# Taking the first four column tiles of a decoder layer K-tile by K-tile, and summing the squares of x on ScalarE

## The chip, the cores and the metric

The kernel runs on one core of one Trainium2 chip. The core has five engines, each with its own instruction stream in a fixed order: PE (TensorE, the matrix unit; PEld is its weight load), DVE (VectorE), ACT (ScalarE), POOL (GpSimd) and SP (SyncE, which here only issues loads). An instruction starts when those ahead of it on its engine have started and the semaphores that it waits for have come. The metric is the device time of one execution in microseconds (us). Profile rows name an instruction by its line in the kernel and by the names of the tiles that it writes and reads.

## The reference, cut to what matters

One layer of a hybrid decoder on x of 256 tokens by 2048 features, all float32:

```python
h = rms_norm(x, ln_mix_pre)
q, k, v, z, xbc, dt_raw = jnp.split(h @ w_in, splits, axis=-1)
attn = moba_attention(q, k, v, rel_bias)
ssm = mamba2_mixer(z, xbc, dt_raw, ...)          # conv of xbc, softplus of dt, chunked state space
x = x + rms_norm(concatenate([attn, ssm]) @ w_out, ln_mix_post)
h = rms_norm(x, ln_ffn_pre)
gate, up = jnp.split(causal_depthwise_conv(h @ w_ffn_up, ...), [FFN_HIDDEN], axis=-1)
x = x + rms_norm((gelu(gate) * up) @ w_ffn_down, ln_ffn_post)
```

`rms_norm` divides each token by the root of the mean of its squares over the 2048 features, plus 1e-6. What matters here is the start: `h @ w_in` for the last 512 columns of xbc (B and C of the state space) and for the 16 columns of dt.

## The kernel before

**Precision.** Each float32 operand of a large product is split into a rounded part (hi, made on ACT) and the exact rest (lo, made on DVE); a product is hi\*hi + lo\*hi + hi\*lo. The weights come in *units* of 128 x 1024 values (512 KB). `Weights.split` loads a unit into `raw` on SP's queue (L64), casts it to `whi` on ACT (L65) and subtracts on DVE for `wlo` (L66). There are four buffers of each; PE must be done with a unit before the cast of the fourth unit after it. `take` hands out the next unit, `fetch` splits one more, and `tick`, once after each unit that PE uses, calls `fetch` and then whatever was put off by `defer(n, ...)` until n more units.

**Activations.** x arrives transposed (`xT`, features on the partitions) in 16 K-tiles of 128 features by 256 tokens (128 KB each), into `xr`. `load_x` splits each, times the norm's weight, into `hT` (ACT L180, DVE L181). The root mean square itself is applied to the products later, so it isn't needed at the start.

**Column tiles.** A column tile is 128 columns of w_in for all 256 tokens in one PSUM bank: for each K-tile a *pair* of matmuls, `whi` against hi and lo together (L186, 512 columns) and `wlo` against hi (L187, 256). The first four tiles (`pab`: two from one PSUM pool, two from the other) are B and C. A unit holds eight K-tiles of one tile. `cols_group` takes the four first units side by side: K-tiles 0 to 3 of each of the four tiles, then 4 to 7 of each. The four units with K-tiles 8 to 15 come after, one tile at a time. Behind the group stand the 32 small matmuls `pd` for dt (L385, L386) on `wd`, the split weights of the 16 time-step columns. The order of instructions on each engine is settled when the program is built, by a scheduler that moves independent work; on PE it has put pd ahead of the second half of the four tiles.

**First loads.** The table `START` sets their order on SP's queue: single K-tiles of x, then pairs, between quarters and halves of the first four units, then `wdr` (time-step weights) and the last K-tiles; small tables (`hv`, `mch`, `cst`, `rb`, `oh`) follow. At the very start PE runs 22 matmuls on zeros (L323, `WARM`).

**Sums of squares.** GpSimd squares `xr` in four groups of four K-tiles into `sq` and adds them up (L372 to L377, nine instructions). When the first unit of v has been used, `token_rms` sums over the partitions with two small matmuls (`pms`, L399), and DVE and GpSimd make 1/sqrt of it (`rsa`, `rsy`, `rsq`, `rr`; `mean_rsqrt`, `rsqrt`).

**After it** come v (`rows_chunk`, matmuls of L266 to L268), eight column tiles of x of the state space, z, attention, the output projection and the feed-forward part; their code is the same in both kernels.

Of the kernel before, what the change touches and what calls it, by code (L numbers as in the profile page):

```python
# [19 lines left out]
P = 128  # L20
# [17 lines left out]
WARM = 22  # L38

# order of the first loads: (x, K-tile, count), (unit, from column block, to column block), time steps  # L40
START = [("x", 0, 1), (0, 0, 2), ("x", 1, 1), (0, 2, 4), ("x", 2, 2), (1, 0, 4), (2, 0, 4), ("x", 4, 2),
         (3, 0, 4), ("x", 6, 2), (0, 4, 8), (1, 4, 8), ("x", 8, 2), (2, 4, 8), (3, 4, 8), ("x", 10, 2),
         ("d",), ("x", 12, 4)]
# [3 lines left out]
# layout of the flat vector of row parameters  # L47
# [7 lines left out]
class Weights:  # L55
    """The weight units in the order of their use, fetched and split ahead of it."""
# [21 lines left out]
    def begin(self, n):  # L78
        """The first n units, for fetching piece by piece."""
        self.fetched = n  # L80
        return [self.tiles(i) for i in range(n)]

    def fetch(self):
        """One more unit into the pool, and those before it that have a place of their own."""
        while self.fetched < len(self.units):
            i = self.fetched
            self.fetched += 1
            self.split(*self.tiles(i), slice(0, UE))
            if i not in self.place:
                return  # L90
# [8 lines left out]
def decoder_layer(ctx, tc, x, xT, win, wdt, wout, wup, wdown, relb, vec, cols, mconv, fconv,  # L99
# [23 lines left out]
    def rsqrt(a, meanwhile=None):  # L123
        """1 / sqrt, element by element of a few columns."""
# [14 lines left out]
    def mean_rsqrt(src, inv):  # L139
        """rsqrt(src * inv + EPS)"""  # L140
# [5 lines left out]
    def early_sum(parts):  # L146
        """The mean square's share of the first three chunks, and EPS."""
# [5 lines left out]
    def late_rsqrt(part, early, meanwhile):  # L153
        """With the share of the last chunk."""
# [4 lines left out]
    def along_tokens(dst, rs):  # L159
        """Columns of one value per token -> dst[every partition, 256 tokens]."""  # L160
# [10 lines left out]
    def split_evac(dst, k, ts, ps):  # L171
        """PSUM -> rounded part and the exact rest, for K-tiles k and token columns ts."""
# [4 lines left out]
    def split_scaled(dst, k, ts, src, w):  # L177
        """The same with a factor per feature."""
# [4 lines left out]
    def cols_part(ps, w, aT, k, j):  # L183
        """K-tile k, the j-th of the unit: ps[128 columns of W, 256 tokens] in two summands."""
# [5 lines left out]
    def cols_tok(ps, w, aT, k, j, t):  # L190
        """The same for one token tile; the last matmul for both, once the bank is begun."""
# [8 lines left out]
    def cols_sum(dst, ps):  # L200
        """Both summands of a tile, and the root mean square of the tokens."""
# [26 lines left out]
    def cols_group(pss, aT):  # L228
        """Tiles side by side, where the activations still come in."""
        w = [ws.take() for _ in pss]  # L230
        for js in (range(4), range(4, 8)):
            for i, ps in enumerate(pss):
                for j in js:
                    cols_part(ps, w[i], aT, j, j)
                if js[-1] == 7:
                    tick()
        for ps in pss:
            w = ws.take()
            for j in range(8):
                cols_part(ps, w, aT, 8 + j, j)  # L240
            tick()

    def cols_pair(pss, aT):
        """Two tiles together, the first token tile ahead of the second, which still comes in."""
# [16 lines left out]
    def rows_part(ps, w, aT, k0, t, first, last):  # L261
        """ps[128 tokens of t, 512 columns] += two K-tiles from k0 on."""
# [8 lines left out]
    def rows_chunk(pss, aT, kts, first=True, last=True, done=None):  # L271
        """The units of the K-tile pairs kts, for both token tiles."""
# [10 lines left out]
    def rows_staggered(pss, aT, kts, done, late, first=True):  # L283
        """The last chunk: eight units token tile by token tile, four of them with their own place."""
# [41 lines left out]
    with ExitStack() as mctx:  # L326
# [3 lines left out]
        with ExitStack() as actx:  # L330
# [3 lines left out]
            # x^T * ln, split; the root mean square is applied to the products  # L334
# [9 lines left out]
            wd = ax.tile([P, KT, 2 * SH], F32R, name="wd")  # L344

            def load_wd():
                nc.sync.dma_start(out=wdr, in_=wdt)
                nc.scalar.copy(wd[:, :, :SH], wdr)
                nc.vector.tensor_tensor(wd[:, :, SH:], wdr, f32(wd[:, :, :SH]), op=ALU.subtract)

            starts = ws.begin(4)
            for kind, *what in START:
                if kind == "d":
                    load_wd()
                elif kind == "x":
                    load_x(*what)
                else:
                    ws.split(*starts[kind], slice(what[0] * P, what[1] * P))
            hv = ax.tile([P, 3, SH], F32, name="hv")
            nc.sync.dma_start(out=hv, in_=row_bcast(V_HEADS, 48))  # L360
            mch = ax.tile([P, 12, 5], F32, name="mch")
            nc.sync.dma_start(out=mch, in_=mconv)
            nc.sync.dma_start(out=cstt, in_=consts)
            rb = ax.tile([33, H], F32, name="rb")
            nc.sync.dma_start(out=rb, in_=relb)
            oh = ax.tile([33, RELW], F32, name="oh", tag="rel", bufs=1)
            nc.sync.dma_start(out=oh, in_=onehot)

            sq = pers.tile([P, 4, 4, S], F32, name="sq", tag="xt", bufs=1)
            for g in range(4):  # L370
                xg = xr[:, g * 4:g * 4 + 4, :]
                nc.gpsimd.tensor_tensor(sq[:, g], xg, xg, op=ALU.mult)  # L372
                if g > 0:
# [597 lines left out]
```

## Time and profile before

| what | value |
|---|---|
| time, median of 3 runs | 1156.71 us (1155.48 to 1157.04) |
| span of the profiled execution | 1153.8 us |
| instructions | 15725 |
| mean granted clock of PE | 0.989 |
| loaded from HBM | 212.39 MB |

The page gives no device time for the profiled execution beside its span; the three timed runs are 1.7 to 3.2 us longer than that span. Of the span's 40 equal slices the first is the one in which PE is least busy apart from the last, and both its clock and the loads are below those of the rest:

```profile
PE   6998999999999899999999999999999999999996
...
POOL 6015122000001500000000000000000000000001
PEclk8999999999999999999999999999999999999999
```

Each digit is the busy share of a slice of 28.8 us in tenths (PEclk: the granted clock in tenths).

### The profile page before, as it was taken

The page shows a single profiled execution, that of the slowest core. Times are in us where ns is not written, and L with a number is a line of the kernel's source. Part 1 is how long each engine was busy: PE and PEld are TensorE (multiplying, and loading weights), DVE is VectorE, ACT ScalarE, POOL GpSimd, SP SyncE. Part 2 cuts the span into 40 slices and gives each one's busy share as a digit, 9 for nine tenths or more (in the row PEclk, how much of TensorE's full clock was granted, in tenths as well). Part 3 has the DMA queues.
Part 4 walks back from the last instruction along what each step waited for, and adds up shares of the span by engine and source line. Part 5 has one row for each costly group of instructions (what it writes and reads, how often), then busy time and mean ns, then how long its engine had stood idle before and what let it go on. Part 6 is the DMA issues. An engine that isn't in the chain of part 4 may idle for free.

```text
span 1153.8 us, 15725 instructions
## 1 busy us (share of the span) xinstructions
PE 1127.2 (98%) x5878; PEld 959.5 (83%) x5878; DVE 806.7 (70%) x1226; ACT 584.0 (51%) x901; POOL 84.9 (7%) x66
## 2 busy tenths in 40 slices
PE   6998999999999899999999999999999999999996
PEld 4877888888888798888888888888888888888885
DVE  8678876766646788778777744447787787775563
ACT  5455544545445466555555544335555555554450
POOL 6015122000001500000000000000000000000001
PEclk8999999999999999999999999999999999999999
DMA  5657644555477455555555555555555555555562
GB/s 196 204 178 243 194 149 147 177 170 165 164 310 237 144 176 198 183 189 192 185 185 189 191 183 190 193 183 187 193 186 184 192 190 183 188 190 188 185 217 73
DMA packets 61189, 215.55 MB, mean 187 GB/s; under 512 B 7247, under 2 KB 8840, under 8 KB 60472
## 3 DMA queue, kind: packets, MB, share of 16 engines
q1 hardware_dynamic: 58408, 204.74, 53.0%
q0 software_dynamic: 1696, 8.60, 2.1%
q10 hardware_dynamic: 1008, 1.20, 0.3%
q8 instruction: 46, 0.75, 0.3%
q14 instruction: 31, 0.25, 0.1%
HBM read 212.39 MB, written 2.13 MB: 186 GB/s over the span
## 4 chain that ended last, share of the span: by engine, by line
PE 93%; DVE 3%; DMA 2%; issue 1%; SPq 0%; POOL 0%; ACT 0%; DVEq 0%; POOLq 0%; ACTq 0%
PE pa L186 36%; PE pa L187 19%; PE pa L266 8%; PE pa L268 8%; PE pa L267 8%; PE ph L267 4%; PE ph L266 4%; PE ph L268 4%; DVE wlo L66 2%; DMA raw<-in_win_dram 1%; PE pa L194 1%; DMA rows<-acd 1%; PE py L557 1%; DVE rows L533 1%; DMA acd<-acr 0%
## 5 line engine op out<-in xcount | busy, mean ns | idle before, releaser
L66 DVE TENSOR_TENSOR wlo<-raw,whi 128x1024 fp32r<-128x1024 f32 (+2 forms) x381 | 472.8, 1243 | 269.1 <-ACT whi L65 268.5
L65 ACT CAST whi<-raw 128x1024 fp32r<-128x1024 f32 (+2 forms) x381 | 395.0, 1038 | 459.4 <-PE pa L186 171.4
L186 PE MATMUL pa<-h,whi 128*128 128x512 f32 x1376 | 483.3, 394 | 0.0
L187 PE MATMUL pa<-h,wlo 128*128 128x256 f32 x1376 | 389.2, 283 | 0.0
L186 PEld LDWEIGHTS pa<-h,whi 128*128 128x128 f32 x1376 | 258.4, 188 | 59.6
L187 PEld LDWEIGHTS pa<-h,wlo 128*128 128x128 f32 x1376 | 258.7, 188 | 0.0
L186 PE MATMUL pa<-hT,whi 128*128 128x512 f32 x416 | 152.0, 404 | 0.0
L187 PE MATMUL pa<-hT,wlo 128*128 128x256 f32 x416 | 119.5, 287 | 7.4 <-DVE wlo L66 7.3
L186 PEld LDWEIGHTS pa<-hT,whi 128*128 128x128 f32 x416 | 79.9, 192 | 17.7
L798 DVE SCALAR_TENSOR_TENSOR cfc<-cfu,fcv,cfc 128x255 f32<-128x255 f32 (+1 forms) x176 | 84.6, 481 | 4.5 <-ACT cfc L796 1.5
L187 PEld LDWEIGHTS pa<-hT,wlo 128*128 128x128 f32 x416 | 80.1, 193 | 8.5 <-DVE wlo L66 8.5
L266 PE MATMUL pa<-whi,gT 128*128 128x512 f32 x176 | 69.4, 395 | 0.0
L268 PE MATMUL pa<-whi,gT 128*128 128x512 f32 x176 | 69.4, 395 | 0.0
L267 PE MATMUL pa<-wlo,gT 128*128 128x512 f32 x176 | 69.4, 394 | 0.0
L127 POOL TENSOR_TENSOR rsy<-rsa,mhalf 128x1 f32<-128x1 f32 (+1 forms) x10 | 7.8, 780 | 788.7 <-DVE rsa L156 732.1
L268 PE MATMUL ph<-whi,gT 128*128 128x512 f32 x160 | 63.1, 395 | 0.0
L267 PE MATMUL ph<-wlo,gT 128*128 128x512 f32 x160 | 63.1, 395 | 0.0
L266 PE MATMUL ph<-whi,gT 128*128 128x512 f32 x160 | 63.1, 395 | 0.0
L796 ACT ACTIVATE cfc<-cfu,fcv 128x256 f32<-128x256 f32 x88 | 52.5, 597 | 1.4 <-DVE cfu L795 1.4
L266 PE MATMUL pa<-whi,hT 128*128 128x512 f32 x128 | 52.4, 410 | 0.0
L267 PE MATMUL pa<-wlo,hT 128*128 128x512 f32 x128 | 50.5, 395 | 0.0
L268 PE MATMUL pa<-whi,hT 128*128 128x512 f32 x128 | 50.5, 395 | 0.0
(237 smaller groups left out, 1234.9 us busy)
## 6 DMA issues: line engine op xcount, KB each, us to landing
raw<-in_wup_dram SPq DMA_DIRECT2D x176, 512.0 KB, 3.5
raw<-in_wdown_dram SPq DMA_DIRECT2D x88, 512.0 KB, 3.5
raw<-in_win_dram SPq DMA_DIRECT2D x84, 512.0 KB, 3.5
raw<-in_wout_dram SPq DMA_DIRECT2D x32, 512.0 KB, 4.3
rows<-acd POOLq DMA_DIRECT2D x4, 512.0 KB, 7.7
xt<-in_x_dram POOLq DMA_DIRECT2D x2, 1024.0 KB, 7.6
raw<-in_win_dram SPq DMA_DIRECT2D x7, 256.0 KB, 6.4
xr<-in_xT_dram SPq DMA_DIRECT2D x5, 256.0 KB, 5.8
```

The source lines that it names most:

```text
L65: nc.scalar.copy(hi[:, s], raw[:, s])
L66: nc.vector.tensor_tensor(lo[:, s], raw[:, s], f32(hi[:, s]), op=ALU.subtract)
L186: nc.tensor.matmul(ps, w[0][:, s], aT[:, k, :, :], start=(k == 0), stop=False)
L187: end[0] = nc.tensor.matmul(ps[:, :S], w[1][:, s], aT[:, k, 0, :], start=False, stop=(k == KT - 1)).ins
L194: nc.tensor.matmul(both, w[0][:, s], aT[:, k, :, tok(t)], start=(t == 0 and k == 0), stop=False)
L266: nc.tensor.matmul(ps, a, w[0][:, s], start=(first and j == 0), stop=False)
L267: nc.tensor.matmul(ps, a, w[1][:, s], start=False, stop=False)
L268: end[0] = nc.tensor.matmul(ps, b, w[0][:, s], start=False, stop=(last and j == 1)).ins
L533: nc.vector.tensor_scalar(seg[:, i, :], seg[:, i, :], nacs[:, t, h:h + 1], 0.0, op0=ALU.add, op1=ALU.min)
L557: nc.tensor.matmul(py[:, i * 64:(i + 1) * 64], rows[:, t, g, i, :], xcs[t, g][:, i * 64:(i + 1) * 64], start=True, stop=True)
L796: nc.scalar.activation(c, u, AF.Identity, scale=wv[:, 2:3], bias=wv[:, 3:4])
L798: nc.vector.scalar_tensor_tensor(c[:, sh:], u[:, :S - sh], wv[:, 2 - sh:3 - sh], c[:, sh:], op0=ALU.mult, op1=ALU.add)
```

## The change

Comments and docstrings are dropped, and line numbers shift by up to eleven. Besides that:

- `cols_first` takes the place of `cols_group`. The first eight units are laid out anew on the host: each holds two K-tiles for all four tiles. PE goes through the units in turn, and in each through K-tile 2u for tiles 0 to 3, then K-tile 2u + 1.
- The first loads follow that order. K-tiles 0 and 1 of x come singly, each ahead of its half of unit 0; units 1 to 3 come whole, each behind its two K-tiles of x. K-tiles 8 and 9 follow; the last six come two at a time behind the fetches of units 4 to 6.
- `load_rest`, after unit 7 is fetched: x again, row by row (tokens on the partitions, two loads of 1 MB), squared in place on ACT with the sum over the features as a second output (`ssx`); then the time-step weights and the small tables.
- GpSimd's nine instructions and the two matmuls of `pms` go; `token_rms` reads `ssx`.
- The warm-up has 16 matmuls in place of 22.

```diff
-WARM = 22
-START = [("x", 0, 1), (0, 0, 2), ("x", 1, 1), (0, 2, 4), ("x", 2, 2), (1, 0, 4), (2, 0, 4), ("x", 4, 2),
...
+WARM = 16
...
-    def cols_group(pss, aT):
-        w = [ws.take() for _ in pss]
-        for js in (range(4), range(4, 8)):
-            for i, ps in enumerate(pss):
-                for j in js:
-                    cols_part(ps, w[i], aT, j, j)
-                if js[-1] == 7:
-                    tick()
-        for ps in pss:
+    def cols_first(pss, aT, after):
+        for u in range(KT // 2):
             w = ws.take()
-            for j in range(8):
-                cols_part(ps, w, aT, 8 + j, j)
+            for j in range(2):
+                for i, ps in enumerate(pss):
+                    cols_part(ps, w, aT, u * 2 + j, j * 4 + i)
             tick()
+            after(u)
...
+            xsq = pers.tile([P, NT, D], F32, name="xsq", tag="xt", bufs=1)
+            ssx = ax.tile([P, NT], F32, name="ssx")
+            def load_rest():
+                for t in range(NT):
+                    nc.sync.dma_start(out=xsq[:, t, :], in_=x[0, tok(t), :])
+                    nc.scalar.activation(xsq[:, t, :], xsq[:, t, :], AF.Square,
+                                         accum_out=ssx[:, t:t + 1])
                 nc.sync.dma_start(out=wdr, in_=wdt)
                 nc.scalar.copy(wd[:, :, :SH], wdr)
                 nc.vector.tensor_tensor(wd[:, :, SH:], wdr, f32(wd[:, :, :SH]), op=ALU.subtract)
+                for dst, src in ((hv, row_bcast(V_HEADS, 48)), (mch, mconv), (cstt, consts),
+                                 (rb, relb), (oh, onehot)):
+                    nc.sync.dma_start(out=dst, in_=src)
...
+            for k in range(2):
+                load_x(k, 1)
+                ws.split(*starts[0], slice(k * 512, k * 512 + 512))
+            for u in range(1, 4):
+                load_x(2 * u, 2)
+                ws.split(*starts[u], slice(0, UE))
+            load_x(8, 2)
+            def after(u):
+                if u < 3:
+                    load_x(10 + 2 * u, 2)
+                elif u == 3:
+                    load_rest()
...
-            for g in range(4):
-                xg = xr[:, g * 4:g * 4 + 4, :]
-                nc.gpsimd.tensor_tensor(sq[:, g], xg, xg, op=ALU.mult)
-                if g > 0:
-                    nc.gpsimd.tensor_tensor(sq[:, 0], sq[:, 0], sq[:, g], op=ALU.add)
...
-                pms = psum("pms")
-                for t in range(NT):
-                    nc.tensor.matmul(pms[:, t:t + 1], s0[:, 0, tok(t)], ones, start=True,
-                                     stop=True)
-                nc.vector.tensor_copy(rr, mean_rsqrt(pms[:, :NT], 1.0 / D))
+                nc.vector.tensor_copy(rr, mean_rsqrt(ssx, 1.0 / D))
...
-    win = np.concatenate([xbc[16:24:2], xbc[17:24:2], rows(w_in[:, 2048:3072]), xbc[:16],
+    win = np.concatenate([rows(w_in[:, 5120:5632]), rows(w_in[:, 2048:3072]), xbc[:16],
```

Where the instructions stand now is shown at three places. The first is PE, right behind the warm-up, before the change (the numbers are those of buffers: 215 to 218 are the banks of the four tiles):

```order
L186 MATMUL pab_215<-hT_100,whi_115 128x512
L187 MATMUL pab_215<-hT_100,wlo_116 128x256
...
L186 MATMUL pab_216<-hT_100,whi_118 128x512
L187 MATMUL pab_216<-hT_100,wlo_119 128x256
...
L186 MATMUL pa_217<-hT_100,whi_121 128x512
L187 MATMUL pa_217<-hT_100,wlo_122 128x256
```

and in the changed kernel (167 to 170 are the banks of the four tiles):

```order
L181 MATMUL pab_167<-hT_94,whi_115 128x512
L181 MATMUL pab_168<-hT_94,whi_115 128x512
L181 MATMUL pa_169<-hT_94,whi_115 128x512
L182 MATMUL pab_167<-hT_94,wlo_116 128x256
L182 MATMUL pab_168<-hT_94,wlo_116 128x256
L182 MATMUL pa_169<-hT_94,wlo_116 128x256
L181 MATMUL pa_170<-hT_94,whi_115 128x512
L182 MATMUL pa_170<-hT_94,wlo_116 128x256
```

Before, four pairs of one tile use one unit, and the next tile needs another; now the first half of one unit serves all four tiles. The pairs of a tile's later K-tiles are left out ahead.

The second place is ACT from the last feature splits on, before the change (`wd` are the time-step weights, `dsb` the copy of pd, `bc` the copies of the finished tiles):

```order
L180 ACTIVATE hT<-xr,cw 128x256 x2
L348 CAST wd<-wdr 128x16x16
L180 ACTIVATE hT<-xr,cw 128x256 x4
L405 ACTIVATE aneg<-hv 128x16
L65 CAST whi<-raw 128x1024
L389 COPY dsb<-pd 32x256
L65 CAST whi<-raw 128x1024 x3
L202 COPY bc<-pab 128x256
L65 CAST whi<-raw 128x1024
L202 COPY bc<-pab 128x256
```

and in the changed kernel, from the last feature split on:

```order
L175 ACTIVATE hT<-xr,cw 128x256 x2
L60 CAST whi<-raw 128x1024
L348 ACTIVATE xsq,ssx<-xsq 128x2048
L197 COPY bc<-pab 128x256 x2
L197 COPY bc<-pa 128x256
L348 ACTIVATE xsq,ssx<-xsq 128x2048
L351 CAST wd<-wdr 128x16x16
L197 COPY bc<-pa 128x256
L394 ACTIVATE aneg<-hv 128x16
L60 CAST whi<-raw 128x1024 x2
L382 COPY dsb<-pd 32x256
```

The cast of the time-step weights has moved from among the feature splits to behind the copies of three finished tiles and the second Square. The third place is DVE at the same point, before the change:

```order
L181 SCALAR_TENSOR_TENSOR hT<-xr,cw,hT 128x256 x2
L349 TENSOR_TENSOR wd<-wdr,wd 128x16x16
L181 SCALAR_TENSOR_TENSOR hT<-xr,cw,hT 128x256 x2
L404 TENSOR_SCALAR mch<-mch 128x60
L181 SCALAR_TENSOR_TENSOR hT<-xr,cw,hT 128x256 x2
L406 TENSOR_SCALAR aneg<-aneg 128x16
L66 TENSOR_TENSOR wlo<-raw,whi 128x1024 x4
L203 TENSOR_TENSOR bc<-pab,bc 128x256
```

and in the changed kernel, from the rest of unit 7 on:

```order
L61 TENSOR_TENSOR wlo<-raw,whi 128x1024
L198 TENSOR_TENSOR bc<-pab,bc 128x256 x2
L198 TENSOR_TENSOR bc<-pa,bc 128x256
L393 TENSOR_SCALAR mch<-mch 128x60
L138 TENSOR_SCALAR rsa<-ssx 128x2
L128 TENSOR_TENSOR rsq<-rsy 128x2
L352 TENSOR_TENSOR wd<-wdr,wd 128x16x16
L198 TENSOR_TENSOR bc<-pa,bc 128x256
L129 TENSOR_TENSOR rsq<-rsq,rsa 128x2
L395 TENSOR_SCALAR aneg<-aneg 128x16
```

The rest of wd now follows the sums of three tiles and the first two steps of the mean's root, of which `rsq` reads what GpSimd has made of `rsa`. On PE pd stands right behind the four tiles, and the first unit of v behind pd. From the third unit of v on the order on every engine is as before.

More of the change, by code (lines that the diff above doesn't have):

```diff
@@ L37 @@
 SPLB = 4
-WARM = 22
-START = [("x", 0, 1), (0, 0, 2), ("x", 1, 1), (0, 2, 4), ("x", 2, 2), (1, 0, 4), (2, 0, 4), ("x", 4, 2),
-         (3, 0, 4), ("x", 6, 2), (0, 4, 8), (1, 4, 8), ("x", 8, 2), (2, 4, 8), (3, 4, 8), ("x", 10, 2),
-         ("d",), ("x", 12, 4)]
+WARM = 16
 C3 = 88 + 24
@@ L344, in decoder_layer @@
             wd = ax.tile([P, KT, 2 * SH], F32R, name="wd")
-            def load_wd():
+            hv = ax.tile([P, 3, SH], F32, name="hv")
+            mch = ax.tile([P, 12, 5], F32, name="mch")
+            rb = ax.tile([33, H], F32, name="rb")
+            oh = ax.tile([33, RELW], F32, name="oh", tag="rel", bufs=1)
+            xsq = pers.tile([P, NT, D], F32, name="xsq", tag="xt", bufs=1)
[5 more added lines that the diff above has]
+                                         accum_out=ssx[:, t:t + 1])
                 nc.sync.dma_start(out=wdr, in_=wdt)
@@ L349, in load_wd @@
                 nc.vector.tensor_tensor(wd[:, :, SH:], wdr, f32(wd[:, :, :SH]), op=ALU.subtract)
+                for dst, src in ((hv, row_bcast(V_HEADS, 48)), (mch, mconv), (cstt, consts),
+                                 (rb, relb), (oh, onehot)):
+                    nc.sync.dma_start(out=dst, in_=src)
             starts = ws.begin(4)
[L352 to L369, printed above, removed]
-            for g in range(4):
-                xg = xr[:, g * 4:g * 4 + 4, :]
-                nc.gpsimd.tensor_tensor(sq[:, g], xg, xg, op=ALU.mult)
-                if g > 0:
-                    nc.gpsimd.tensor_tensor(sq[:, 0], sq[:, 0], sq[:, g], op=ALU.add)
-            s0 = sq[:, 0]
-            nc.gpsimd.tensor_tensor(s0[:, :2], s0[:, :2], s0[:, 2:], op=ALU.add)
-            nc.gpsimd.tensor_tensor(s0[:, 0], s0[:, 0], s0[:, 1], op=ALU.add)
+            for k in range(2):
[10 more added lines that the diff above has]
+                    load_rest()
             pab = [psum("pab") for _ in range(2)] + [col_psum() for _ in range(2)]
-            cols_group(pab, hT)
+            cols_first(pab, hT, after)
             pd = psum("pd")[:2 * SH, :S]
```

## The prediction

> **What bounds the kernel now.** I read the page first for the engine that is busy throughout, then the table by stage, then the timelines of PE, DVE and ACT where PE has gaps. In the tables the columns are stage, its length, busy time (and count) of PE, weight load, DVE, ACT and POOL, granted clock, DMA share, GB/s.
>
> ```profile
> PE 1127.2 (98%) x5878; PEld 959.5 (83%) x5878; DVE 806.7 (70%) x1226; ACT 584.0 (51%) x901; POOL 84.9 (7%) x66
> ...
> 0.00:47.78 47.78, 36.79 (x183) 30.42 (x184) 35.58 (x40) 21.76 (x40) 18.91 (x13) 0.86 0.58 201
> 47.78:96.00 48.22, 48.22 (x221) 38.44 (x220) 34.53 (x90) 23.56 (x35) 10.22 (x11) 1.00 0.65 207
> 96.00:110.00 14.00, 10.79 (x50) 8.72 (x49) 13.08 (x21) 8.01 (x12) 9.53 (x6) 0.88 0.55 190
> ```
>
> PE is the bound of nearly the whole program: between 47.78 and 96 us it never rests and has its full clock. Two stages stand out: the first 47.78 us, where it is idle for 11.0 us and has a mean clock of 0.86, and a smaller hole at 96 to 110 us. The change lies wholly in the first, so that stage is where the time must come from.
>
> ```profile
> 9.15 0.79 PE L186 MATMUL pab<-hT,whi 128*128 128x512 f32 x1 [2.65 <-DVE hT L181]
> ...
> 13.14 0.39 PE L186 MATMUL pa<-hT,whi 128*128 128x512 f32 x1
> ...
> 13.49 0.39 PE L186 MATMUL pa<-hT,whi 128*128 128x512 f32 x1
> ...
> 19.03 0.51 PE L187 MATMUL pab<-hT,wlo 128*128 128x256 f32 x1 [3.04 <-DVE wlo L66]
> 19.34 0.63 PE L186 MATMUL pab<-hT,whi 128*128 128x512 f32 x1
> ...
> 19.98 0.63 PE L186 MATMUL pab<-hT,whi 128*128 128x512 f32 x1
> ...
> 27.99 0.58 PE L187 MATMUL pa<-hT,wlo 128*128 128x256 f32 x1 [4.20 <-DVE wlo L66]
> ...
> 32.83 0.27 PE L385 MATMUL pd<-hT,wd 128*32 128x256 f32 x1
> ...
> 36.54 0.39 PE L186 MATMUL pab<-hT,whi 128*128 128x512 f32 x1
> ...
> 47.78 0.40 PE L266 MATMUL pa<-whi,hT 128*128 128x512 f32 x1
> ```
>
> PE waits three times, 2.65, 3.04 and 4.20 us, each time for DVE. The start of one pair (hi and lo matmul) to the next is 13.49 - 13.14 = 0.35 us normally, but 19.98 - 19.34 = 0.64 us after a gap: the clock is halved. The stage below, after the third gap, shows it in the clock's column (0.50 for 4.7 us). The 64 pairs of the first four tiles would need 64 x 0.35 = 22.5 us and the time-step products pd 36.54 - 32.83 = 3.7 us; they end at 47.78.
>
> ```profile
> 28.00:32.70 4.70, 4.70 (x15) 4.03 (x16) 4.70 (x11) 0.00 (x0) 0.52 (x1) 0.50 0.58 220
> ...
> L181 DVE SCALAR_TENSOR_TENSOR hT<-xr,cw,hT 128x256 fp32r<-128x256 f32 x5 | 9.7, 1975 | 0.0
> L66 DVE TENSOR_TENSOR wlo<-raw,whi 128x512 fp32r<-128x512 f32 x5 | 8.7, 1775 | 0.0
> ...
> L66 DVE TENSOR_TENSOR wlo<-raw,whi 128x1024 fp32r<-128x1024 f32 x7 | 8.4, 1220 | 6.7 <-ACT whi L65 6.7
> L181 DVE SCALAR_TENSOR_TENSOR hT<-xr,cw,hT 128x256 fp32r<-128x256 f32 x6 | 2.6, 474 | 0.0
> ...
> L203 DVE TENSOR_TENSOR bc<-pab,bc 128x256 f32<-128x256 f32 x2 | 0.8, 416 | 0.0
> ...
> L349 DVE TENSOR_TENSOR wd<-wdr,wd 128x256 fp32r<-128x256 f32 x1 | 0.4, 414 | 0.0
> ...
> 11.32 2.54 POOL L372 TENSOR_TENSOR sq<-xr 128x1024 f32<-128x1024 f32 x1 [2.50 <-DMA xr<-in_xT_dram]
> ...
> 27.47 1.05 POOL L377 TENSOR_TENSOR sq<-sq 128x256 f32<-128x256 f32 x1
> ```
>
> These are DVE's groups, first for 12 to 29 us, then (from the third on) for 29 to 48 us. The same feature split takes 1975 ns on average in the first and 474 in the second; the weight split of half the size takes longer (1775) than the whole one later (1220). The first stretch is that in which GpSimd squares and adds x, almost without a break from 11.32 to 28.5 us. So the root of the second and third gap is GpSimd's work, which slows the two splits DVE owes to PE.
>
> **The change, part by part.** (1) *GpSimd's nine instructions go.* DVE's splits fall to 474 and 1220 ns. (2) *K-tile by K-tile.* Unit u now holds K-tiles 2u and 2u+1 for all four tiles, so a unit and two K-tiles of x feed 8 pairs, 8 x 0.35 = 2.81 us of PE. Against it, per unit:
>
> ```profile
> L65 ACT CAST whi<-raw 128x1024 fp32r<-128x1024 f32 x8 | 8.2, 1048 | 6.6 <-DMA raw<-in_win_dram 5.3 <-PE pa L186 1.3
> L180 ACT ACTIVATE hT<-xr,cw 128x256 fp32r<-128x256 f32 x16 | 7.3, 501 | 3.2 <-DMA xr<-in_xT_dram 2.5 <-DMA cw<-in_cols_dram 0.5
> L65 ACT CAST whi<-raw 128x512 fp32r<-128x512 f32 x7 | 4.1, 611 | 0.9 <-DMA raw<-in_win_dram 0.8
> L348 ACT CAST wd<-wdr 128x256 fp32r<-128x256 f32 x1 | 0.4, 389 | 0.0
> ...
> 3.20 0.51 ACT L180 ACTIVATE hT<-xr,cw 128x256 fp32r<-128x256 f32 x1 [0.52 <-DMA cw<-in_cols_dram]
> ...
> 8.49 1.31 ACT L65 CAST whi<-raw 128x512 fp32r<-128x512 f32 x2 [0.80 <-DMA raw<-in_win_dram]
> ...
> 12.40:15.70 3.30, 3.30 (x21) 2.87 (x19) 3.30 (x2) 3.15 (x8) 3.22 (x2) 1.00 1.04 374
> ```
>
> ACT 1.05 + 2 x 0.50 = 2.05 us, DVE 1.22 + 2 x 0.47 = 2.16 us, and the loads, 768 KB at 374 GB/s (the rate of 12.4 to 15.7 us, when the queue is full), 2.1 us. All lie under 2.81 us, so from some unit on PE is the bound again. The question is only when that starts. By 8.48 us (ACT then begins the cast it had waited for) the old order had landed four K-tiles of x, and the first halves of units 0 and 1: 1024 KB. The new order needs 1536 KB for the same point, units 0 and 1 whole and four K-tiles. The other 512 KB at 374 GB/s take 1.4 us: unit 1 is there at **9.9 us**, cast at 10.95, its rest split at 12.2. If the whole 1536 KB came at 374 GB/s behind the first K-tile (3.2 us, ACT's first split), it would be 3.2 + 1.44 MB/374 GB/s = 7.1; if the slow start (1024 KB in 8.48 us) went on, 12.7. I take 9.9, since 374 is the rate the loads had from then on. PE has unit 0's weights from about 5 us and is done with it (2.81 us) near 8, so it idles for some 3 us as in the rows above and then gets the half clock for 3 us or more. Unit 1 has four hi matmuls behind it at 12.2; what is left (4 lo at 0.12, 4 pairs at 0.35, 1.9 us) costs 2.9 with the clock half for the first two: 15.1. Six units follow: 15.1 + 6 x 2.81 = **32.0 us** for the end of the fourth tile.
>
> (3) *Sums of squares on ACT.* Here the new order takes back part of it. ACT runs the second Square behind the first three copies of the finished tiles, and the split of the time-step weights wd stands behind it: on DVE it comes after the mean's first steps (rsa, then rsq, which waits for GpSimd's power). PE stands at pd until wd is there.
>
> ```profile
> L202 ACT COPY bc<-pab 128x256 f32<-128x256 f32 x2 | 0.7, 362 | 1.2 <-PE pab L187 1.2
> ...
> L169 ACT ACTIVATE junk<-xt 128x512 f32<-128x512 f32 x8 | 5.0, 631 | 2.2 <-DVE xt L732 2.1
> ...
> L169 ACT ACTIVATION_READ_ACCUMULATOR junk<-xt 128x1 f32 x8 | 1.5, 188 | 0.0
> ...
> 51.10 0.16 DVE L143 TENSOR_SCALAR rsa<-pms 128x2 f32<-128x2 f32 x1 [0.60 <-PE pms L399]
> ...
> 52.08 0.16 DVE L133 TENSOR_TENSOR rsq<-rsy 128x2 f32<-128x2 f32 x1 [0.82 <-POOL rsy L127]
> 52.28 0.16 DVE L134 TENSOR_TENSOR rsq<-rsq,rsa 128x2 f32<-128x2 f32 x1
> ...
> 50.56 0.50 PE L399 MATMUL pms<-cst,sq 128*128 128x1 f32 x4
> 50.92 0.48 PE L266 MATMUL pa<-whi,hT 128*128 128x512 f32 x1
> ```
>
> A Square of 128x2048 isn't in the trace. From 512 elements (631 ns) and the slope of the casts, (1048 - 611)/512 = 0.85 ns an element, it is 0.63 + 1536 x 0.85 = 1.9 us, with the accumulator's reading 0.19 some 2.1; between 1.75 (slope alone) and 2.7 (four of 631 and a reading). The third tile ends 0.35 us ahead of the fourth; the third copy ends at +0.05; Square to +2.15; rsa to rsq's start 52.08 - 51.10 = 0.98, rsq 0.20, wd 0.41, and 0.1 for the signals: PE starts pd **3.85 us** after the fourth tile, where before it waited for nothing. pd ends at 32.0 + 3.85 + 3.7 = 39.55. A gap of this length halves the clock too; of 3 to 4.7 us at the half clock a part falls into the gap itself, and half of the rest, about 1.3 us, is lost: **40.85 us** against 47.78, a gain of 6.9. The two matmuls of pms go as well, 50.92 - 50.56 = 0.36 us on PE's path: 7.3 us in all.
>
> The Trainium skill ("TensorE: Matmul & The Clock Gate", HAM oscillation) speaks of idle gaps over about 3.4 us as those that throttle the clock; the rows above differ, since 2.65 and 3.04 us were enough. What hangs on it is a rival below.
>
> At no cost: the copies of the tiles, aneg and the next casts are queued behind the second Square on ACT, but unit 8 is cast at 2.15 + 0.39 + 0.36 + 1.05 and the small aneg, about +4.2 us, and split by DVE after wd, the last tile's sum (0.42), five small steps (0.2 each) and its own 1.22, at about +6.4. PE needs it after pd, at +7.5; the cover is 1 us, and what exceeds it is paid one for one. The 2 MB of x in rows are loaded between units 7 and 8. Up to the end of the second megabyte there are 8.39 MB, 22 us at 374 GB/s behind the first K-tile; with the 2.8 us lost at the start it lands at 28, 4 us before ACT comes to it. Six warm-up matmuls fewer (0.21 us each) end at 4.5 us, and the first weights come at about 5.
>
> **The rivals.** *Loads land early:* units 0 and 1 by 7.1 us, the rest of unit 1 starts at 9.4 with no gap worth a throttle, the fourth tile ends at 9.4 + 1.9 + 6 x 2.81 = 28.2, pd with its gap and the clock's 1.3 us at 37.05, a gain of 10.7 and the 0.36: 1145.6. For it: larger loads; against: in the old order the rate was low for 8 us whatever was queued. *No throttle by short gaps:* if only an idle stretch that fills a whole period counts, both gaps pass at full clock, 1.0 + 1.3 us less: 1147.1. Three rows speak against it. The rule of the Trainium skill named above, on that page, would give this. *The slow start goes on:* unit 1 at 12.4, everything 2.8 us later: 1152.2. *Paid back later:* the hole at 96 to 110 us is a wait for DVE at the end of a chain through the rows of decays, sent by GpSimd's queue:
>
> ```profile
> 103.47 0.39 PE L187 MATMUL pa<-hT,wlo 128*128 128x256 f32 x1 [3.08 <-DVE wlo L66]
> ...
> 36.50:47.80 11.30, 11.30 (x67) 9.91 (x66) 7.96 (x9) 7.17 (x10) 0.00 (x0) 1.00 0.62 209
> ```
>
> If that chain ended at its old time, the 3.08 us would grow by what was gained: no change, 1156.7. Against it: the chain begins with matmuls at a fixed place behind pd and would move with PE. *Slower:* the second megabyte of x lands late. ACT, wd, pd and with them everything wait for it. The 8.26 MB between the first K-tile (3.2 us) and its end would need 39.5 us at the 209 GB/s of 36.5 to 47.8 us and land at 42.7; Square, mean and wd (2.1 + 1.7) and pd make 50.2, with the clock halved (1.7 of 3.4 us) 51.9: 4.1 later, less 0.36, 1160.4. It decides from a mean rate below about 230 GB/s on. Against it: 209 is what was asked for there, and with a full queue there were 374.
>
> **How the numbers follow.** The sum is made against the profiled span (1153.8 us); the page gives no more of that execution, and the three runs lie 1.7 to 3.2 us above, so I take the difference off the median: 1156.7 - 7.3 = **1149.4**. Forecast (1147.5 to 1151.5) 0.53; early loads 0.15; no throttle 0.08; slow start 0.14; paid back 0.06; slower 0.04. The range 1145.0 to 1153.4 reaches over early loads and slow start and the bounds of Square; it leaves out the last two and the outer tails. About 0.2%, 2.3 us, is what can be told from no change: faster 0.89, same 0.07, slower 0.04.
>
> **What would show it.** DVE's feature splits near 0.48 us throughout and no PE wait for them after unit 1; pairs 0.35 us apart from about 15 us on; fourth tile done near 32; one PE wait of about 3.85 us for wd, by DVE, ahead of pd, and a half clock after it; the first row chunk near 41; the hole near 100 us moved by about 7 us and as long as before. Wrong would be PE waits for loads in units 2 to 7, or a Square that waits for its DMA.

## The result, and the profile after

The changed kernel takes 1146.86 us (median of 4 runs, 1146.03 to 1149.01) where before took 1156.60 (1155.48 to 1157.04): ratio 0.9918, 95% interval 0.9904 to 0.9932, 9.7 us less. Forecast were 1149.4 us and a range from 1145.0 to 1153.4. The profiled execution took 1146.03 us with a span of 1144.3.

The page of the changed kernel and its table by stage come first; the columns are those of the prediction (stage, length, busy time and count of PE, weight load, DVE, ACT, POOL, granted clock, DMA share, GB/s).

```profile
PE 1122.8 (98%) x5868; PEld 956.4 (84%) x5868; DVE 793.7 (69%) x1222; ACT 587.7 (51%) x901; POOL 66.2 (6%) x57
...
0.00:38.00 38.00, 31.70 (x167) 25.45 (x168) 21.91 (x43) 24.51 (x39) 0.91 (x5) 0.96 0.80 288
38.00:88.00 50.00, 50.00 (x232) 39.99 (x230) 36.63 (x84) 24.89 (x36) 11.34 (x11) 1.00 0.71 228
88.00:102.00 14.00, 11.21 (x56) 9.52 (x54) 13.05 (x22) 8.65 (x12) 7.74 (x5) 0.88 0.52 168
```

GpSimd has almost left the first stage (0.91 us busy, 18.91 before), PE is idle there for 38.00 - 31.70 = 6.3 us in place of 11.0, and the hole near 95 us is still there, with the same clock of 0.88. PE's timeline of the changed kernel, its waits and the ends of the pieces:

```profile
7.45 0.73 PE L181 MATMUL pab<-hT,whi 128*128 128x512 f32 x2 [0.41 <-ACT whi L60]
...
10.30 0.73 PE L181 MATMUL pab<-hT,whi 128*128 128x512 f32 x2 [1.16 <-ACT whi L60]
...
30.31 0.28 PE L182 MATMUL pa<-hT,wlo 128*128 128x256 f32 x1
34.14 0.42 PE L378 MATMUL pd<-hT,wd 128*32 128x256 f32 x1 [3.55 <-DVE wd L352]
...
39.12 0.62 PE L257 MATMUL pa<-whi,hT 128*128 128x512 f32 x2
...
93.68 0.39 PE L182 MATMUL pa<-hT,wlo 128*128 128x256 f32 x1 [2.79 <-DVE wlo L61]
```

The three waits of 2.65, 3.04 and 4.20 us have become two short ones for ACT's casts and a new one of 3.55 for wd. The four tiles end at 30.43 (the last lo matmul takes 0.12 of PE's time), and the first row chunk begins at 39.12, 8.66 earlier than before. From the first row chunk to the end of the wait at the hole there are 54.56 us where there were 55.69, 1.13 less. Behind the hole 0.29 us are lost again, and so the spans differ by 9.5. DVE's groups from 10 to 30 us, and then ACT and DVE ahead of pd:

```profile
L61 DVE TENSOR_TENSOR wlo<-raw,whi 128x1024 fp32r<-128x1024 f32 x7 | 8.6, 1225 | 1.5 <-ACT whi L60 1.5
L176 DVE SCALAR_TENSOR_TENSOR hT<-xr,cw,hT 128x256 fp32r<-128x256 f32 x12 | 5.2, 478 | 0.0
```

```profile
30.28 0.37 ACT L197 COPY bc<-pa 128x256 f32<-128x256 f32 x1
30.55 1.91 ACT L348 ACTIVATE xsq<-xsq 128x2048 f32<-128x2048 f32 x1
32.36 0.19 ACT L348 ACTIVATION_READ_ACCUMULATOR xsq<-xsq 128x1 f32 x1
32.46 0.39 ACT L351 CAST wd<-wdr 128x256 fp32r<-128x256 f32 x1
...
33.58 0.16 DVE L128 TENSOR_TENSOR rsq<-rsy 128x2 f32<-128x2 f32 x1 [0.82 <-POOL rsy L122]
33.66 0.43 DVE L352 TENSOR_TENSOR wd<-wdr,wd 128x256 fp32r<-128x256 f32 x1
35.63 1.22 DVE L61 TENSOR_TENSOR wlo<-raw,whi 128x1024 fp32r<-128x1024 f32 x1 [0.33 <-issue]
```

The splits have their undisturbed times (478 and 1225 ns). Behind the third copy stands the second Square (1.91 and 0.19 us), then wd, and on DVE wd's rest waits behind the mean's chain: this is the wait of 3.55 us. Unit 8's split ends at 36.85, ahead of PE's need at 39.12.

### The profile page after: what moved, and what is told of

Same layout as the page of the kernel before. It is cut to its first block, busy times and chain, and to the rows that moved or that the text cites. A ratio compares the mean times of both kernels' runs of the same rounds, so it can differ in the third digit from the quotient of the medians.

```text
span 1144.3 us, 15694 instructions
## 1 busy us (share of the span) xinstructions
PE 1122.8 (98%) x5868; PEld 956.4 (84%) x5868; DVE 793.7 (69%) x1222; ACT 587.7 (51%) x901; POOL 66.2 (6%) x57
## 4 chain that ended last, share of the span: by engine, by line
PE 92%; DMA 3%; DVE 3%; issue 1%; SPq 0%; POOL 0%; ACT 0%; DVEq 0%; POOLq 0%; ACTq 0%
PE pa L181 35%; PE pa L182 18%; PE pa L257 8%; PE pa L259 8%; PE pa L258 8%; PE ph L259 4%; PE ph L258 4%; PE ph L257 4%; DVE wlo L61 1%; DMA raw<-in_win_dram 1%; DMA xsq<-in_x_dram 1%; PE pa L189 1%; DMA rows<-acd 1%; PE py L546 1%; DVE rows L522 1%
## 5 line engine op out<-in xcount | busy, mean ns | idle before, releaser
L61 DVE TENSOR_TENSOR wlo<-raw,whi 128x1024 fp32r<-128x1024 f32 (+1 forms) x377 | 468.3, 1243 | 265.8 <-ACT whi L60 264.6
L60 ACT CAST whi<-raw 128x1024 fp32r<-128x1024 f32 (+1 forms) x377 | 394.6, 1048 | 451.2 <-PE pa L181 170.3
```

The costliest lines, as they stand in the source:

```text
L60: nc.scalar.copy(hi[:, s], raw[:, s])
L61: nc.vector.tensor_tensor(lo[:, s], raw[:, s], f32(hi[:, s]), op=ALU.subtract)
```

## The experiments

The theory was that GpSimd's work caused the gaps, that the second Square between the copies gives part of the gain back, and that a rest of PE costs a half clock behind it. The main rival was the order of tiles and loads as the cause.

All of them in one table. Three columns are worked out from windows of the profile with the clock, each for the one execution that was profiled: how long the clock was halved in the first 45 us, at the hole, and near 390 us, far behind the change. Elsewhere it was full, but for the last 3 to 6 us of the program, in which PE has no work left. Before, measured beside these kernels, had medians of 1156.33 to 1156.76.

| kernel | median us | row chunks begin | half clock to 45 us | at the hole | near 390 us |
|---|---|---|---|---|---|
| before (profile) | 1156.60 | 47.78 | 13.7 | 3.4 | 3.4 |
| changed | 1146.86 | 39.12 | 3.4 | 3.4 | 3.4 |
| changed again | 1147.40 | 39.26 | 3.4 | 3.4 | 3.4 |
| K-tile order, GpSimd's squares | 1155.01 | 45.84 | 6.8 | 3.4 | 6.8 |
| old order, squares on ACT | 1144.04 | 34.19 | 3.4 | 0 | 6.8 |
| changed, Squares ahead of the copies | 1142.76 | 34.43 | 0 | 3.4 | 3.4 |
| old order, Squares ahead | 1144.15 | 34.81 | 0 | 6.8 | 3.4 |
| changed, pd's wait filled | 1146.86 | 37.96 | 0 | 6.8 | 3.4 |
| changed, 22 warm-up matmuls | 1149.30 | 39.38 | 3.4 | 6.8 | 3.4 |
| changed, hole filled | 1146.05 | 39.48 | 3.4 | 0 | 6.8 |
| changed, both filled | 1144.76 | 37.98 | 0 | 0 | 6.8 |
| Squares ahead, hole filled | 1141.65 | 34.08 | 0 | 0 | 6.8 |
| 22 warm-up, hole filled | 1146.81 | 40.32 | 6.8 | 0 | 3.4 |
| old order, Squares ahead, hole filled | 1141.85 | 33.41 | 0 | 0 | 3.4 |

The last column is a caution for the two ahead of it. No experiment touches that place, and PE has two waits there in every kernel, 2.38 to 2.40 and then 0.57 to 1.03 us; yet one stretch at half clock belongs to them in nine profiles and a double one in five. First the repeat of the changed kernel, then the changed kernel with the hole filled:

```profile
391.67 0.66 PE L747 MATMUL pxt<-cst,hl 128*128 128x128 f32 x4 [2.38 <-POOL hl L726]
393.35 4.84 PE L189 MATMUL pa<-h,whi 128*128 128x256 f32 x26 [1.03 <-DVE h L170]
...
393.40:396.70 3.30, 3.30 (x15) 3.30 (x16) 3.19 (x9) 2.34 (x8) 0.97 (x2) 0.50 0.65 184
...
389.92 0.66 PE L750 MATMUL pxt<-cst,hl 128*128 128x128 f32 x4 [2.40 <-POOL hl L729]
391.60 5.91 PE L189 MATMUL pa<-h,whi 128*128 128x256 f32 x26 [1.03 <-DVE h L170]
...
390.70:397.40 6.70, 5.80 (x27) 5.80 (x28) 6.53 (x14) 3.29 (x9) 1.92 (x2) 0.50 0.39 139
```

The waits are alike, and the stretches aren't. The executions of one kernel differ too: the old order with squares on ACT had a mean granted clock of 0.996 in those of 1143.30 and 1143.37 us, and of 0.994 in those of 1144.71 and 1145.03. So a difference of 1 to 2 us that rests on the number of stretches in a single profile isn't shown to belong to the kernel. One that rests on a wait that went or came is.

**The changed kernel again**, as the measure for the others.

> The changed kernel once more, as the measure for the others of this series. Expected 1146.9 us +- 1, its fourth column tile done at about 30.4 us, pd begun at 34.1, the first row chunk at 39.1.

1147.40 us (1146.22 to 1147.93), ratio 0.9914 (0.9901 to 0.9928). The start is the same within 0.14 us. The hole isn't: from the first row chunk to its end it takes 55.82 us here and 54.56 in the first profile, at waits of 0.72 and 3.06 us against one of 2.79. So the 1.1 us gained at the hole in the first profile aren't the change's.

**The K-tile order alone**, GpSimd squaring and adding as before:

```diff
-                    nc.scalar.activation(xsq[:, t, :], xsq[:, t, :], AF.Square,
-                                         accum_out=ssx[:, t:t + 1])
...
+                nc.gpsimd.tensor_tensor(sq[:, g], xg, xg, op=ALU.mult)
+                if g > 0:
+                    nc.gpsimd.tensor_tensor(sq[:, 0], sq[:, 0], sq[:, g], op=ALU.add)
```

> The changed kernel with the sums of squares back on GpSimd (from the transposed x, four groups as they land), the K-tile order kept. Theory (the gain comes from taking GpSimd's work away from beside DVE's splits): DVE's splits fall to about a third of their speed while GpSimd runs, for some 19 us; of the 12 to 14 us lost DVE has 5 to spare, so the fourth tile ends near 38 to 39, with clock losses; pd waits for nothing. First row chunk at 42 to 46 us, time 1150 to 1153. Rival (the K-tile order makes PE the bound, GpSimd's work hides behind it): the fourth tile ends near 31 and pd follows at once, first row chunk at about 34.5, time about 1142.

1155.01 us (1153.89 to 1156.11), ratio 0.9984 (0.9975 to 0.9993): even later than the 1150 to 1153 expected. DVE's timeline of this kernel, GpSimd's rows beside the two slow splits and around its pause, and PE's longest wait:

```profile
16.81 2.91 DVE L61 TENSOR_TENSOR wlo<-raw,whi 128x1024 fp32r<-128x1024 f32 x1
...
22.56 1.22 DVE L61 TENSOR_TENSOR wlo<-raw,whi 128x1024 fp32r<-128x1024 f32 x1
...
26.14 3.38 DVE L61 TENSOR_TENSOR wlo<-raw,whi 128x1024 fp32r<-128x1024 f32 x1
...
16.57 2.08 POOL L347 TENSOR_TENSOR sq<-xr 128x1024 f32<-128x1024 f32 x1
18.72 3.24 POOL L349 TENSOR_TENSOR sq<-sq 128x1024 f32<-128x1024 f32 x1
24.05 1.89 POOL L347 TENSOR_TENSOR sq<-xr 128x1024 f32<-128x1024 f32 x1 [2.09 <-DMA xr<-in_xT_dram]
26.02 2.42 POOL L349 TENSOR_TENSOR sq<-sq 128x1024 f32<-128x1024 f32 x1
...
19.78 0.50 PE L182 MATMUL pab<-hT,wlo 128*128 128x256 f32 x2 [4.31 <-DVE wlo L61]
```

The weight split takes 2.91 and 3.38 us with GpSimd at work and 1.22 in the pause that GpSimd makes from 21.96 to 24.05, where it waits for x. PE waits 4.31 and 2.68 us for it. The K-tile order without the moved squares is worth 1.75 us (1156.76 less 1155.01), not the gain. The Trainium skill ("SBUF — State Buffer", Who interferes with whom) says that a DVE instruction with two SBUF inputs contends with a GpSimd instruction that reads SBUF, and that the later of the two is held up wholly. The rows agree: each of the two slow splits starts just behind a GpSimd instruction (at 16.81 behind 16.57, at 26.14 behind 26.02) and ends 1.1 us after that one's end (18.65 and 28.44), close to the 1.22 us that a split takes undisturbed; in the pause it loses nothing.

**The squares alone**, the old order of tiles and loads kept; the load of x in rows and the Squares stand behind the first four tiles' units, and wd stays among the feature splits, with pd in the midst of the tiles:

```diff
-            cols_group(pab, hT)
+            cols_group(pab, hT, load_squares)
...
-                nc.vector.tensor_copy(rr, mean_rsqrt(pms[:, :NT], 1.0 / D))
+                nc.vector.tensor_copy(rr, mean_rsqrt(ssx, 1.0 / D))
```

> The kernel before with only the sums of squares moved to ScalarE and the row-wise load (behind unit 7), the old tile and load order kept. Theory: PE's second and third wait (3.04 and 4.20 us) and their half clocks go, the first (2.65 us, loads) stays; the second Square stands ahead of the cast of unit 8, which costs a wait of about 2 us behind the fourth tile. First row chunk at 39 to 41 us, time 1147 to 1150. Rival (the order is what counts): the waits stay for loads and splits in another order, first row chunk at 45 or later, time 1153 to 1156.

1144.04 us (1143.30 to 1145.03), ratio 0.9885 (0.9870 to 0.9900): faster than the whole change, and below the 1147 to 1150 expected. PE has one wait of 0.98 us at the start, where 2.65 had been expected to stay, and none to 33.7. The row chunk then waits for unit 8. First PE, then ACT, then DVE:

```profile
34.19 0.72 PE L267 MATMUL pa<-whi,hT 128*128 128x512 f32 x2 [0.50 <-ACT whi L65]
36.37 0.50 PE L268 MATMUL pa<-wlo,hT 128*128 128x512 f32 x1 [1.46 <-DVE wlo L66]
...
31.19 1.92 ACT L376 ACTIVATE xsq<-xsq 128x2048 f32<-128x2048 f32 x1
33.01 0.19 ACT L376 ACTIVATION_READ_ACCUMULATOR xsq<-xsq 128x1 f32 x1
33.10 1.03 ACT L65 CAST whi<-raw 128x1024 fp32r<-128x1024 f32 x1
...
35.09 1.23 DVE L66 TENSOR_TENSOR wlo<-raw,whi 128x1024 fp32r<-128x1024 f32 x1
```

The stage behind these waits, by windows:

```profile
36.90:40.20 3.30, 3.30 (x9) 2.51 (x9) 3.23 (x4) 0.34 (x1) 0.00 (x0) 0.50 0.76 211
```

Unit 8's cast stands behind the second Square here, because no pd lies between the tiles and the row chunk: the two waits make 1.96 us, and 3.4 us at half clock follow.

**The Squares and wd ahead of the copies** in the changed kernel, by the order on ScalarE alone:

```diff
-                cols_sum(bc[:, i, :], pab[i])
+                with tc.issue_after(last[0]):
+                    cols_sum(bc[:, i, :], pab[i])
```

(`last` holds the latest of the Squares and wd's cast.)

> The changed kernel with one more rule of order: on ScalarE the second Square and the cast of the time-step weights are issued ahead of the copies of the four finished tiles. Theory (pd's wait of 3.7 us is only the queue order, since the row-wise x has landed by about 27 us): pd follows the fourth tile at once and at full clock, 3.7 + 1.4 = 5.1 us less: first row chunk at about 34.1, time about 1141.8. Rival (the wait moves on to the copies or to unit 8, or the row-wise load is what is late): pd or unit 8 waits 2 us or more, time 1143.5 to 1146.

1142.76 us (1141.99 to 1145.62), ratio 0.9880 (0.9864 to 0.9896). ACT and PE of it:

```profile
27.17 1.92 ACT L350 ACTIVATE xsq<-xsq 128x2048 f32<-128x2048 f32 x1 [0.53 <-DMA xsq<-in_x_dram]
...
29.08 0.39 ACT L353 CAST wd<-wdr 128x256 fp32r<-128x256 f32 x1
...
30.76 0.30 PE L380 MATMUL pd<-hT,wd 128*32 128x256 f32 x1 [0.36 <-DVE wd L354]
...
34.43 0.62 PE L257 MATMUL pa<-whi,hT 128*128 128x512 f32 x2
```

The wait falls from 3.54 to 0.36 us, no half clock follows it, and the row chunks begin 4.8 us earlier than in the repeat; the median falls by 4.6. That is what the place of the second Square, and of wd's cast behind it, costs the changed kernel.

**The same in the old order** (the copies' edit in the kernel with the squares alone):

> The kernel with the old tile and load order and the sums of squares on ScalarE, with both Squares issued ahead of the copies of the four tiles. Theory (what the first of these kernels lost behind the four tiles, 0.5 + 1.46 us of waits and 3.4 us at half clock, is the queue order on ScalarE, and the K-tile order is worth nothing once GpSimd is out of the way): first row chunk at about 33.6 us with no wait, 3.5 us less than without the rule of order, about 1140.4, and 1 to 3 us under the K-tile order with the same rule. Rival (the K-tile order pays once the queue order is right in both): 1142.8 or more.

1144.15 us (1141.35 to 1144.45), ratio 0.9889 (0.9876 to 0.9902). A miss: the waits ahead of the row chunk are gone, which begins at 34.81, yet the median stands as without the edit. The stage behind the hole by windows shows what the profiled execution (1144.37 us) lost there:

```profile
90.10:96.80 6.70, 5.78 (x18) 5.01 (x19) 5.78 (x10) 5.03 (x7) 4.54 (x2) 0.50 0.51 162
```

A double stretch at half clock, 6.8 us, stands where the profile of the kernel without the edit has none. That one has in its place 3.4 us behind the row chunk's waits and 6.8 near 390 us, against 3.4 there in this one: 10.2 us of half clock in each. That the edit brings on the double stretch isn't shown; another execution of this kernel took 1141.35 us at a higher mean clock (0.995, and 0.994 in the profiled one).

**pd's wait filled** with 33 matmuls of zeros into an unused bank, so that PE doesn't rest:

```diff
             cols_first(pab, hT, after)
+            with tc.issue_after(end[0]):
+                for _ in range(33):
+                    fill = nc.tensor.matmul(idle[:, :S], zero[:, :P], zero, start=True, stop=True).ins
...
+            with tc.issue_after(fill):
```

> The changed kernel with 33 matmuls on zeros (256 columns, about 0.107 us each at full clock) between the fourth tile and pd, so that PE is busy while it would wait for the time-step weights. Theory (the wait halves the clock, and that costs pd some 1.4 us beside the wait itself): pd starts at about 34.1 us as before, runs at 0.116 us a matmul, first row chunk at about 37.8 in place of 39.1 to 39.3; time 1.4 us under the changed kernel, about 1145.7. Rival (the half clock after the wait has another cause, or pd's matmuls are not bound by the clock): no change, 1147.1.

1146.86 us (1145.67 to 1147.17), ratio 0.9915 (0.9902 to 0.9928), so no gain that could be told, the time that the rival named. PE's timeline of this kernel; then the stage behind the hole by windows, of this kernel and (last fence) of the changed kernel:

```profile
30.53 3.78 PE L376 MATMUL idle<-zero 128*128 128x256 bf16 x33
...
34.23 0.30 PE L382 MATMUL pd<-hT,wd 128*32 128x256 f32 x1
...
37.96 0.39 PE L257 MATMUL pa<-whi,hT 128*128 128x512 f32 x1
```

```profile
93.60:99.50 5.90, 5.90 (x19) 5.03 (x20) 4.99 (x9) 5.18 (x8) 4.54 (x2) 0.50 0.67 187
```

```profile
94.90:98.30 3.40, 3.40 (x13) 2.92 (x12) 2.49 (x3) 3.40 (x6) 3.40 (x2) 0.50 0.67 228
```

At its place the filling did what the theory said: no half clock, pd in 3.73 us, row chunks 1.2 to 1.3 us earlier. Behind the hole, whose wait is 3.07 us as in the repeat, PE then worked 5.9 us at half clock in place of 3.4: 1.25 us lost there. So the rival's reason fell, at pd, and only its time came out. That the filling brings on the double stretch isn't shown; over all its executions the mean clock was no lower than the repeat's (0.993 to 0.995 against 0.992 to 0.994).

**Warm-up of 22 matmuls** in the changed kernel (`WARM = 22`):

> The changed kernel with 22 warm-up matmuls as before, in place of 16. Theory (unit 0 lands behind the warm-up, and the clock is up in either case): the six matmuls hide behind the loads, within 0.3 us of the changed kernel, 1147.1. Rival (the shorter warm-up lets PE start earlier and is part of the gain): 0.5 to 1.3 us slower, 1147.6 to 1148.4.

1149.30 us (1147.39 to 1152.55, 6 runs), ratio 0.9941 (0.9929 to 0.9954): 1.9 to 2.4 us more than with 16, which neither view had expected. Yet the row chunks begin at 39.38, only 0.1 to 0.3 us later. What differs in the profile lies at the hole again: waits of 0.70 and 0.79 us ahead of it, where the repeat has one of 0.72, and a double stretch at half clock behind it.

The last runs filled the hole itself, ahead of the unit whose rest DVE has late, with 28 matmuls that add zeros to the tile:

```diff
+            if u == 1:
+                for _ in range(fill):
+                    nc.tensor.matmul(ps[:, :S], zero[:, :P], zero, start=False, stop=False)
```

**The hole filled in the changed kernel:**

> The changed kernel, with 28 matmuls of zeros put into the hole near 94 us (ahead of the second unit of the first column tile after the row chunks), so that PE never rests there. Theory: the hole's wait itself (3.07 us, DVE) stays as elapsed time, but the half clock after it goes. The profiled executions of the changed kernel had 3.4 us at half clock there, 1.7 us lost: 1145.4 us, and no clock below 1.00 after 60 us. Rival: what follows the hole isn't decided by PE's rest, and the filling does nothing or costs its own time: 1147 to 1150.

1146.05 us (1144.19 to 1146.78), ratio 0.9911 (0.9896 to 0.9926): 0.8 to 1.35 us less than the two measurements without it, of 1.7 expected, and within the spread of its own four runs. The clock stays at 1.00 from 60 to 125 us. It does so at the hole in all five kernels with the filling, and in one of the nine without it: the half clock there comes with PE's rest. "No clock below 1.00 after 60 us" did not come true, though: near 390 us this profile has the double stretch, 6.8 us, where the changed kernel had 3.4. The 28 matmuls at 0.117 us take 3.3 us, somewhat more than the wait they fill.

**Both filled:**

> Both waits filled with zeros: the one ahead of pd and the hole near 94 us. Theory: filling the first alone brought the first row chunk from 39.2 to 38.0 us and lost that again because two stretches at half clock (6.9 us) followed the hole instead of one (3.4 us). With both filled the first gain must show: 1146.9 - 3.0 = 1143.9, some 1.3 below the kernel with the hole alone filled. Rival: filling the first wait gains nothing lasting: the same time as the kernel with the hole alone filled.

1144.76 us (1144.49 to 1145.67), ratio 0.9904 (0.9889 to 0.9919). The start and the hole of this kernel by windows:

```profile
30.00:38.00 8.00, 8.00 (x70) 6.98 (x70) 5.31 (x17) 6.17 (x11) 0.71 (x1) 1.00 0.33 125
80.00:100.00 20.00, 20.00 (x115) 16.70 (x114) 19.08 (x31) 11.62 (x16) 12.57 (x8) 1.00 0.71 226
```

Full clock in both. The 1.3 us that the first filling had gained and lost now show in the median, 1144.76 against 1146.05, as expected, though the ranges of the two kernels overlap and 1143.9 was not reached. Both profiles have the double stretch near 390 us, so they compare well: 1144.82 against 1146.78, of which 1.5 us are there when the row chunks begin (37.98 against 39.48).

**The Squares ahead and the hole filled:**

> Squares and wd ahead of the tile copies on ScalarE, and the hole near 90 us filled with zeros. Theory: the two gains add: 1142.8 - 1.6 = 1141.2 us, 4.3 below the kernel with the hole alone filled, the fastest of all here. Rival: 1142.8 or more.

1141.65 us (1140.65 to 1142.06), ratio 0.9877 (0.9860 to 0.9893), the lowest of all; 4.4 below the kernel with the hole alone filled, as expected.

**22 warm-up matmuls and the hole filled:**

> The changed kernel with 22 warm-up matmuls in place of 16, and the hole filled. Theory: the warm-up itself costs nothing (the first row chunk began at 39.38 us against 39.12 and 39.26); its 2 us came from the two stretches at half clock after the hole and about 0.8 us of small waits ahead of it. With the hole filled 1149.3 - 3.0 = 1146.3, within 1 us of the kernel with 16 warm-up matmuls and the hole filled. Rival: the longer warm-up costs 2 us by itself, 1147.5 or more, 2 us above that kernel.

1146.81 us (1145.04 to 1147.57), ratio 0.9918 (0.9903 to 0.9933), 0.8 us over the kernel with 16. This profile shows a double stretch at half clock around pd (6.8 us; 3.4 with 16), and the row chunks begin 0.84 us later for it. The other profile with 22 has a single one there, so that isn't shown to be the warm-up's doing. With the hole filled 0.8 of the 2 us are left, within the spread of the runs.

**The old order, the Squares ahead and the hole filled:**

> The order of tiles and loads of before, the sums of squares on ScalarE ahead of the tile copies, and the hole near 90 us filled with zeros: the same as the run that gave 1141.65, but without the K-tile order. Theory: with GpSimd silent the old order starves PE no more than the new one, and this kernel's loss was the two stretches at half clock after the hole (from 91.0 to 96.8 us, 2.9 us lost): 1144.15 - 2.9 = 1141.3, within 1 us of 1141.65, so the K-tile order is worth nothing by itself once the sums are moved. Rival: the K-tile order is worth its 1.75 us here as well: 1143.4 or more.

1141.85 us (1141.10 to 1142.52), ratio 0.9877 (0.9860 to 0.9893): the same as the K-tile order with these edits (1141.65). With GpSimd out of the way no worth of the K-tile order can be told; the 1.75 us of the rival did not show, and less than 1 us couldn't be seen beside ranges of 1.4.

## Why the prediction was right, and where it was off

*The root.* Right, and shown from both sides: without GpSimd's nine instructions the splits take 478 and 1225 ns, with them the K-tile order keeps PE waits of 4.31 and 2.68 us. The prediction took the change as a whole, though, and didn't ask what each half is worth: the squares alone bring 12.7 us (1156.76 less 1144.04), the K-tile order alone 1.75, and both together 9.4 to 9.7. In the old order pd stood in the midst of the tiles with wd long split; the changed kernel has put wd behind the squares and pd behind the tiles, where the wait falls on PE.

*The start (term 2).* Here the sum was 1.6 us too high: the fourth tile was put at 32.0 and ended at 30.43. Two steps failed. "Unit 1 is there at 9.9": its cast began at 9.20. And PE was to idle "for some 3 us as in the rows above" with a half clock behind it; it waited 0.41 and 1.16 us, and no half clock followed. Unit 0 itself was slower than I had it (its second half was cast at 6.77 and done near 9.1, not near 8), so that the same lateness of the loads left less rest. And the 2.65 us before were not the loads' alone, as the sum had them: GpSimd's first square stood beside the splits that PE waited for. DVE and GpSimd before, then DVE in the old order with squares on ACT:

```profile
7.33 2.17 DVE L181 SCALAR_TENSOR_TENSOR hT<-xr,cw,hT 128x256 fp32r<-128x256 f32 x2 [1.59 <-ACT hT L180]
6.93 1.90 POOL L372 TENSOR_TENSOR sq<-xr 128x1024 f32<-128x1024 f32 x1 [6.48 <-DMA xr<-in_xT_dram]
...
7.25 0.88 DVE L181 SCALAR_TENSOR_TENSOR hT<-xr,cw,hT 128x256 fp32r<-128x256 f32 x2 [1.16 <-ACT hT L180]
```

Without GpSimd the same two splits take 1.3 us less, and PE's wait falls from 2.65 to 0.98 us in the old order of loads. From unit 2 on the 2.81 us per unit held: 30.43 less six units is 13.57, against 15.1 in the prediction.

*Squares on ACT (term 3).* Right in each step: Square and reading 2.1 us (1.91 and 0.19), pd 3.71 us behind the fourth tile (3.85), pd with its half clock 4.98 us (5.0). Moving the Squares and wd ahead gave 4.6 us back, and filling PE's rest let the row chunks begin 1.2 to 1.3 us earlier: close to the wait and the clock's share as they stood in the sum, 3.85 and 1.3.

*The hole.* It was to be "moved by about 7 us and as long as before". It moved by 9.8 us in the first profile and 8.4 in the repeat, since the start gained more. As long as before is right for the repeat (55.82 us from the first row chunk to the end of its wait, 55.69 before); the first profile was 1.1 shorter. The profiled executions differ by 9.5 us where 7.3 were forecast: 1.7 more at the start, 0.8 more at the hole (1.13 less the 0.36 of pms that the sum had) and 0.3 less behind it. The repeat gained 8.2, and there only the start was better than the sum. So the share of the hole is chance, of one execution.

*The costs put at nothing* stayed hidden: unit 8's split ended 2.3 us before its need (the prediction had 1), the second megabyte of x was there at 27.2 in the run where ACT came to it early (28), and with 22 warm-up matmuls pd begins at the same 34.14 us as with 16. The cover of unit 8 is real: with pd elsewhere, 1.96 us of waits appeared at the row chunk.

*The rivals.* The measured 1146.86 lies within the range, but below the 1147.5 to 1151.5 that had got a chance of 0.53. Two rivals are nearer in time. "No throttle by short gaps" (1147.1) is the nearest, by luck: it fell at pd, where 3.4 us at 0.50 followed a wait of 3.55, and the first waits, 0.41 and 1.16 us in place of some 3, were too unlike the forecast to test it. "Loads land early" (1145.6) is only half there: unit 1 landed at 9.2, not by 7.1, and yet no half clock followed the first waits. The slow start did not go on (unit 1 was forecast at 12.4 for that), and the second megabyte of x, which "slower" put at 42.7, was there at 27.2. "Paid back later" fell: the hole moved with PE.

What stays open: why DVE is late at the hole by almost the same 3.07 us in nearly every kernel wasn't tried, and neither was what sets none, one or two stretches at half clock.

## What to carry to other kernels

Take a change of two halves apart before crediting either: here the half that looked like the plan (order of tiles and loads) was worth nothing that could be told beside the other, and the move of the other onto ScalarE cost 4.6 us by its place in that engine's queue. What is put on an engine's queue near a hand-over belongs ahead of the work that waits for PE, not between. Before a variant is judged by 1 or 2 us, look at the clock behind every rest of PE, to the end of the program: the stretches at half clock behind a rest differ from one execution to the next, and a single profile can put down to a variant what isn't its own. Filling such a rest with zeros takes them away at that place.

## What the runs showed of the hardware that was not expected

While PE has work, the half clock comes in stretches of 3.4 us or twice that, never between, in these profiles: 3.4 after waits of 2.79 and 3.55 us in the changed kernel, 6.8 after 3.07 us in three others, none after 3.06 in the old order with squares on ACT. Near 390 us waits of 2.38 and 1.03 us in one profile and of 2.40 and 1.03 in another met 3.4 and 6.8. The same wait thus costs nothing, 1.7 or some 3 us. It doesn't take one long rest: 0.50 and 1.46 us, 0.7 apart, halved the clock, while single waits of 1.53, 1.35 and 1.16 us didn't. The Trainium skill ("TensorE: Matmul & The Clock Gate", What's actually happening) describes activity windows of 3413 ns that run freely and don't start with the kernel; stretches in whole multiples of 3.4 us and the different outcomes of one wait agree with it. That only rests over about 3.4 us halve the clock, as the section named in the prediction (HAM oscillation) has it, doesn't agree with these rows.
